# Splitting the preparation of a seven-product unit among the down chunks of a feed-forward kernel

## The chip, the core and the metric

The kernel runs on one core of one Trainium2 chip. The metric is the device time of one execution in microseconds (us); less is better. The core has TensorE (PE in the profile, with PEld for its weight loads), VectorE (DVE), ScalarE (ACT), GpSimd (POOL) and SyncE (SP, which here only issues DMA transfers). Every engine works through its own queue strictly in the order in which the program was written down; a semaphore wait at the head of a queue holds up all that stands behind it.

## What is computed

One encoder layer over 512 tokens with a model width of 1024. Two feed-forward half steps (hidden width 2816) stand around an attention mixer, and a gated embedding closes the layer:

```
h = h + 0.5 * swiglu(rms_norm(h, g_ffn1), w_ffn1_gate, w_ffn1_up, w_ffn1_down)
u = rms_norm(h, g_mix) @ w_in
...                                       # two kinds of attention on parts of u
h = h + concat([o_mla, o_diff]) @ w_out
h = h + 0.5 * swiglu(rms_norm(h, g_ffn2), w_ffn2_gate, w_ffn2_up, w_ffn2_down)
gate = sigmoid(rms_norm(h, g_ple_in) @ w_ple_gate + b_ple_gate)
h = h + gate * rms_norm(p @ w_ple_proj, g_ple_out)

swiglu(u, wg, wu, wd) = (silu(u @ wg) * (u @ wu)) @ wd
```

All weights come in float32. The kernel keeps float32 accuracy by splitting each operand into a high part and a low part and making three matmuls for each product (lines 391, 392 and 393: high by high, high by low, low by high).

## The kernel before

**Feed-forward, groups.** A feed-forward step works through its 22 hidden blocks of 128 in four groups (`FGROUPS`): a first, *plain* group of 4 blocks and three groups of 6. Every group makes its hidden blocks `ht` (gate product, silu, times up product) and then runs the *down* stage: eight products `ps_d`, one for each output block m, each added into `h[m]` at line 677.

**Units.** In the groups of 6 the gate and up products are not made directly: `seven` multiplies a 2 by 2 arrangement of weight blocks with 2 by 2 parts of the activations in seven products of 12 matmuls each (three partial sums in PSUM, `r1`, `r2`, `r3`) instead of eight. One `Unit` holds the weights of one such call. Units alternate: one for the gate of a pair of hidden blocks, one for the up. A group has 6 units, the kernel 36. A unit is prepared in 11 steps:

- loads on SP: `rb` and `rc` (`load_b`), then `ra` (`load_a`);
- `sums` (lines 157 and 158): two transfers issued by POOL, which add another weight block from memory onto `rb` and `rc`;
- `cast_a`, `cast_b` (ACT, lines 162, 166): high parts of `xa` and `xb`; `low_a`, `low_b` (DVE, line 97): their low parts. `low_b` also has POOL add `rb` into `ra` in two steps (lines 174, 175), which can't begin before `low_a` has read `ra`;
- `cast_c`, `low_c` for `xc`; `cast_s0`, `low_s0`, `cast_s1`, `low_s1` (ACT lines 187, 193, DVE line 97) for the two halves of `xs`, made from the summed `ra`.

The first product of `seven` needs the first half of `xs`: its high part for the matmuls of lines 391 and 392, its low part for line 393.

**Order.** The list `items` holds all weights in the order of use: the plain weights as `Chunk` (one load, one cast, one low part), the units, and the down chunks behind the units of their group. `advance` takes the next step of the front item. It is called by `steps(n)` inside `seven`, between its products (1, 2, 2, 1, 1, 2, 2 steps, so 11 for each unit), and by `slot(us)` elsewhere, until a budget of time is spent, a unit is ready, or the buffers (`held`, three of each kind) are full. Loads run ahead of the steps through three raw buffers (`RAWS`). So a step's place in the queues is where `steps` or `slot` stood when it was taken. In the down stage of the kernel before, `slot` and then `build(2)` stand behind the update of `h[m]` at line 677. `build` hands out the preparation of the activations (`Forms`: `y` at line 499, the sums at lines 506 to 515, `sa` and `fm` pages), which has to be over before the first unit.

**End.** After the last group eight gate chunks (`ps_pg`) follow, whose results `evac_gate` finishes on DVE and ACT. Before each group of `evac_gate` calls stands a `slot`, partly behind them.

## Time and profile before

| | |
|---|---|
| time, median of 3 runs | 1118.36 us (1117.15 to 1119.0) |
| time of the profiled execution | 1119.93 us |
| span of the profiled execution (first to last instruction) | 1118.2 us |
| PE busy | 1039.0 us (93% of the span) |
| DVE, ACT, POOL busy | 769.2, 522.5, 324.9 us |
| mean granted TensorE clock | 0.984 of full speed |
| chain that ended last, by engine | PE 55%, DVE 21%, issue 7%, ACT 5%, DMA 3% |

The profile is of one execution. Its time is 1.6 us above the median of the three timed runs and 1.7 us above its own span. PE is idle for 79 us of the span; a busy PE counts matmuls from their start to their modelled end, which overlap.

### The profile page before, as it was taken

What the parts mean: (1) busy time and instruction counts of PE and PEld (TensorE: products, weight loads), DVE (VectorE), ACT (ScalarE), POOL (GpSimd) and SP (SyncE); (2) the same over time, 40 slices, a digit from 0 to 9 for tenths busy, and PEclk for the clock granted to TensorE, in tenths of its full rate; (3) what the DMA queues carried; (4) which work ended last, traced back from release to release, by engine and by line L of the source; (5) the groups of instructions that cost most, each with busy time, mean ns of one, the idle gap of its engine ahead of it and who ended that gap; (6) DMA issues with size and microseconds to landing.
All of it is one profiled execution on the core that took longest, in us unless ns stands there. A gap on an engine that the chain in (4) does not pass through costs nothing.

```text
span 1118.2 us, 16005 instructions
## 1 busy us (share of the span) xinstructions
PE 1039.0 (93%) x6100; PEld 904.9 (81%) x6100; DVE 769.2 (69%) x1277; ACT 522.5 (47%) x891; POOL 324.9 (29%) x283
## 2 busy tenths in 40 slices
PE   8978899889988999999999999978898889989998
PEld 7768888878888898876667888778887888888777
DVE  7796754775567558888798763977745674677765
ACT  6443442443344346568687552534433442344432
POOL 1133312440433110026553231234325330452000
PEclk9998999999999999999999999989999999999999
DMA  7254635554554443222112122255465635555231
GB/s 244 79 136 128 141 114 144 148 132 149 131 145 112 136 147 129 76 81 77 51 40 70 39 94 76 85 132 145 119 214 138 152 109 142 151 141 180 84 105 67
DMA packets 50463, 133.76 MB, mean 120 GB/s; under 512 B 5873, under 2 KB 6897, under 8 KB 50385
## 3 DMA queue, kind: packets, MB, share of 16 engines
q1 hardware_dynamic: 37008, 106.88, 28.9%
q0 software_dynamic: 11792, 23.47, 11.9%
q10 hardware_dynamic: 1584, 2.39, 0.6%
q8 instruction: 48, 0.79, 0.3%
q14 instruction: 31, 0.25, 0.1%
HBM read 126.02 MB, written 6.29 MB: 118 GB/s over the span
## 4 chain that ended last, share of the span: by engine, by line
PE 55%; DVE 21%; issue 7%; ACT 5%; DMA 3%; POOL 1%; DVEq 0%; SPq 0%; ACTq 0%; POOLq 0%
PE r L393 7%; PE r L391 5%; PE r L392 5%; PE ps_d L391 5%; PE ps_d L392 5%; PE ps_d L393 5%; DVE xb L97 3%; DVE q L559 3%; PE ps_in L392 2%; PE ps_in L391 2%; PE ps_in L393 2%; DVE xs L97 2%; DVE xc L97 2%; DVE hl L97 2%; PE ps_wo L391 1%
## 5 line engine op out<-in xcount | busy, mean ns | idle before, releaser
L97 DVE TENSOR_TENSOR hl<-raw,hl 128x1024 fp32r<-128x1024 f32 (+4 forms) x110 | 121.4, 1114 | 47.0 <-ACT hl L124 44.8
L174 POOL TENSOR_TENSOR ra<-ra,rb 128x512 f32<-128x512 f32 x36 | 76.7, 2130 | 249.5 <-DVE xa L97 247.0
L124 ACT CAST hl<-raw 128x1024 fp32r<-128x1024 f32 (+2 forms) x104 | 96.5, 942 | 108.3 <-DMA raw<-in_wst_dram 35.0
L393 PE MATMUL ps_d<-ht,hl 128*128 128x512 f32 x352 | 137.4, 390 | 2.3 <-DVE hl L97 2.3
L392 PE MATMUL ps_d<-ht,hl 128*128 128x512 f32 x352 | 137.3, 390 | 0.2
L391 PE MATMUL ps_d<-ht,hl 128*128 128x512 f32 x352 | 137.3, 390 | 0.0
L391 PE MATMUL r<-sa,xa 128*128 128x256 f32 x288 | 84.2, 292 | 0.0
L392 PE MATMUL r<-sa,xa 128*128 128x256 f32 x288 | 84.2, 292 | 0.0
L393 PE MATMUL r<-sa,xa 128*128 128x256 f32 x288 | 84.0, 292 | 0.0
L391 PE MATMUL r<-fm,xb 128*128 128x256 f32 x288 | 82.0, 285 | 0.0
L392 PE MATMUL r<-fm,xb 128*128 128x256 f32 x288 | 81.7, 284 | 0.0
L393 PE MATMUL r<-fm,xb 128*128 128x256 f32 x288 | 81.5, 283 | 0.0
L393 PEld LDWEIGHTS ps_d<-ht,hl 128*128 128x128 f32 x352 | 66.1, 188 | 17.6 <-DVE hl L97 4.0
L97 DVE TENSOR_TENSOR xs<-ra,xs 128x512 fp32r<-128x512 f32 x72 | 52.0, 725 | 40.8 <-ACT xs L193 22.1
L391 PE MATMUL r<-fm,xs 128*128 128x256 f32 x144 | 44.4, 309 | 37.2 <-ACT xs L187 37.2
L392 PEld LDWEIGHTS ps_d<-ht,hl 128*128 128x128 f32 x352 | 66.1, 188 | 14.5 <-DVE ht L94 1.0
L391 PEld LDWEIGHTS ps_d<-ht,hl 128*128 128x128 f32 x352 | 66.1, 188 | 13.4
L555 DVE TENSOR_TENSOR q<-r,q 128x256 f32<-128x256 f32 x36 | 15.3, 425 | 79.1 <-PE r L393 75.8
L393 PE MATMUL r<-fm,xs 128*128 128x256 f32 x144 | 46.3, 321 | 24.7 <-DVE xs L97 24.7
L391 PEld LDWEIGHTS r<-fm,xs 128*128 128x128 f32 x144 | 28.8, 200 | 42.2 <-ACT xs L187 42.1
L157 POOL DMA_DIRECT2D rb<-in_wst_dram x36 | 31.8, 884 | 91.0 <-DMA rb<-in_wst_dram 61.1
L392 PEld LDWEIGHTS r<-sa,xa 128*128 128x128 f32 x288 | 58.1, 202 | 0.0
(335 smaller groups left out, 3150.4 us busy)
## 6 DMA issues: line engine op xcount, KB each, us to landing
raw<-in_wst_dram SPq DMA_DIRECT2D x52, 512.0 KB, 3.5
rb<-in_wst_dram SPq DMA_DIRECT2D x36, 512.0 KB, 4.1
ra<-in_wst_dram SPq DMA_DIRECT2D x36, 512.0 KB, 3.4
raw<-in_wst_dram SPq DMA_DIRECT2D x48, 384.0 KB, 3.5
rc<-in_wst_dram SPq DMA_DIRECT2D x36, 256.0 KB, 4.4
rb<-in_wst_dram POOLq DMA_DIRECT2D x36, 256.0 KB, 4.5
rc<-in_wst_dram POOLq DMA_DIRECT2D x36, 256.0 KB, 5.6
h<-in_xT_dram SPq DMA_DIRECT2D x8, 256.0 KB, 4.4
```

Source lines behind the costliest of these rows:

```text
L97: nc.vector.tensor_sub(dst_l, src, dst_h.bitcast(F32))
L124: nc.scalar.copy(self.hl[:, 0, :self.n], self.raw[:, :self.n])
L157: nc.gpsimd.dma_start(out=self.rb[:, self.LO], in_=self.s1[:, self.HI], accum_op=ALU.add)
L174: nc.gpsimd.tensor_add(ra[:, LO], ra[:, LO], self.rb[:, LO])
L391: MM(ps, lhsT=wh, rhs=ah, start=start, stop=False, **kw)
L392: MM(ps, lhsT=wh, rhs=al, start=False, stop=False, **kw)
L393: MM(ps, lhsT=wl, rhs=ah, start=False, stop=stop, **kw)
L555: nc.vector.tensor_add(q2[:, lo], r3[:, lo], q1[:, lo])
L559: nc.vector.tensor_sub(q1[:, hi], q1[:, lo], q2[:, hi])
```

## The change

It has five parts.

1. The order of a unit's steps becomes `cast_a`, `low_a`, `cast_b`, `low_b` (before: both casts, then both low parts).
2. The first unit of a group is taken apart: its loads and `sums` (one `Part`) and its next four steps (a second `Part`) stand among the down chunks of the group before, with cut 2, 2 in the plain group and 6, 7 in the others; the other six steps stay behind the chunks. The source addresses are taken when an item is made, so that the order of use no longer sets them.
3. `slot` goes on over a ready unit if the next step is the `sums` of a whole unit. In the `seven` of a group's first unit the steps therefore begin with `cast_a` of the second, and all stand one step earlier.
4. In the down stage `slot` stands ahead of the update of `h[m]`, and `build` is spread out (one step in each of the three early products of the plain group, one for m below 2, then two).
5. At the end, four of the eight gate chunks use the other kind of buffer, and `slot(3.0)` stands ahead of the `evac_gate` calls.

```diff
     class Unit:
-            self.steps = [(0.0, self.sums, 0), (0.1, self.cast_a, 1), (0.1, self.cast_b, 1), (1.2, self.low_a, 0),
+            self.steps = [(0.0, self.sums, 0), (0.1, self.cast_a, 1), (1.2, self.low_a, 0), (0.1, self.cast_b, 1),
                           (1.2, self.low_b, 0), (0.1, self.cast_c, 0), (0.7, self.low_c, 0),
...
+    class Part:
+
+        def __init__(self, unit, n, loads):
+            self.which = unit.which
+            self.loads = [unit.loads.pop(0) for _ in range(loads)]
+            self.steps = [unit.steps.pop(0) for _ in range(n)]
+
     def ffn_items():
...
+                down = [Chunk(2 * n * P) for m in range(0, KT, 2)]
+                cut = 2, 2
             else:
+                items.extend(first_unit if u == 0 else Unit(1 - u % 2) for u in range(n))
+                down = [Chunk(n * P, 1 if m < KT // 2 else 0) for m in range(KT)]
+                cut = 6, 7
+            if gi < len(FGROUPS) - 1:
+                first_unit = Unit(1)
+                early_ = Part(first_unit, 1, 2), Part(first_unit, 4, 0)
+                down.insert(cut[1], early_[1])
+                down.insert(cut[0], early_[0])
+            items.extend(down)
...
-    items.extend(Chunk(BLK) for _ in range(KT))
+    items.extend(Chunk(BLK, 1 if m < KT // 2 else 0) for m in range(KT))
...
-        while st["time"] > 0 and not any(isinstance(it, Unit) for it in ready) and advance():
+        while st["time"] > 0 and (not any(isinstance(it, Unit) for it in ready)
+                                  or isinstance(items[-1], Unit) and len(items[-1].steps) == 11) and advance():
             pass
...
                     slot(1.3)
+                    build(1)
...
+                slot(0.0 if plain and m < 2 else 0.68 * n - (2.2 if gi == len(FGROUPS) - 1 else 0.75))
                 nc.vector.scalar_tensor_tensor(out=h[m], in0=ps, scalar=0.5, in1=h[m],
                                                op0=ALU.mult, op1=ALU.add)
...
-                slot(0.0 if plain and m < 2 else 0.68 * n - (2.2 if last else 0.75))
-                build(2)
+                build(1 if m < 2 else 2)
...
+        slot(3.0)
         if m == 1:
             rbc = row_bcast(r4)
-            slot(1.2)
         for e in pend:
             evac_gate(*e)
         pend = []
-        slot(3.0)
```

The lines of the changed kernel inside `ffn` and `seven` are numbered 17 higher than those of the kernel before (555 becomes 572); those of `Unit` and of the helpers stay.

**DVE, an up unit (the second of a pair).** Of the kernel before, from the result of its third product (line 555) to the first half of `xs` of the next unit:

```order
L555 TENSOR_TENSOR q_848<-r_846,q_847 128x256
L97 TENSOR_TENSOR xa<-ra,xa 128x1024
L97 TENSOR_TENSOR xb<-rb,xb 128x1024
L558 TENSOR_TENSOR q_849<-r_845,q_848 128x256
L559 TENSOR_TENSOR q_847<-q_847,q_848 128x256
L604 TENSOR_TENSOR a_719<-r_844,a_719 128x256
L97 TENSOR_TENSOR xc<-rc,xc 128x512
L565 TENSOR_TENSOR q_848<-r_846,q_847 128x256
L604 TENSOR_TENSOR a_719<-q_848,a_719 128x256
L97 TENSOR_TENSOR xs<-ra,xs 128x512
```

The same place in the changed kernel:

```order
L97 TENSOR_TENSOR xa<-ra,xa 128x1024
L572 TENSOR_TENSOR q_850<-r_848,q_849 128x256
L97 TENSOR_TENSOR xb<-rb,xb 128x1024
L575 TENSOR_TENSOR q_851<-r_847,q_850 128x256
L576 TENSOR_TENSOR q_849<-q_849,q_850 128x256
L97 TENSOR_TENSOR xc<-rc,xc 128x512
L621 TENSOR_TENSOR a_721<-r_846,a_721 128x256
L582 TENSOR_TENSOR q_850<-r_848,q_849 128x256
L621 TENSOR_TENSOR a_721<-q_850,a_721 128x256
L97 TENSOR_TENSOR xs<-ra,xs 128x512
```

The low part of `xa` stands ahead of the third product's result, and that of `xc` ahead of the fifth's; the first half of `xs` stands where it stood.

**ACT, a gate unit (the first of a pair).** Of the kernel before, from the cast of `xc` to the second half of `xs` (lines 597 and 599 are the silu of the three partial results):

```order
L180 CAST xc<-rc 128x512
L597 ACTIVATE a_719<-r_720 128x256
L597 ACTIVATE a_719<-q_724 128x256
L187 CAST xs<-ra 128x512
L599 ACTIVATE q_725<-q_725 128x512
L193 CAST xs<-ra 128x512
```

The same place in the changed kernel:

```order
L180 CAST xc<-rc 128x512
L614 ACTIVATE a_721<-r_722 128x256
L187 CAST xs<-ra 128x512
L614 ACTIVATE a_721<-q_726 128x256
L193 CAST xs<-ra 128x512
L616 ACTIVATE q_727<-q_727 128x512
```

Each cast of `xs` stands one silu earlier.

**DVE, the end of the plain group.** Of the kernel before; `hl` is the low part of a down chunk, lines 584 to 588 make the last hidden block, whose low part is `ht`:

```order
L97 TENSOR_TENSOR hl<-raw,hl 128x1024
L584 TENSOR_TENSOR a<-ps_g,rbc 128x512
L587 TENSOR_TENSOR v<-ps_u,rbc 128x512
L588 TENSOR_TENSOR v<-a,v 128x512
L94 TENSOR_TENSOR ht<-v,ht 128x512
```

The same place in the changed kernel:

```order
L97 TENSOR_TENSOR hl<-raw,hl 128x1024
L97 TENSOR_TENSOR xa<-ra,xa 128x1024
L97 TENSOR_TENSOR xb<-rb,xb 128x1024
L601 TENSOR_TENSOR a<-ps_g,rbc 128x512
L604 TENSOR_TENSOR v<-ps_u,rbc 128x512
L605 TENSOR_TENSOR v<-a,v 128x512
L94 TENSOR_TENSOR ht<-v,ht 128x512
```

The low parts of `xa` and `xb` of the next group's first unit stand ahead of the last hidden block of the plain group. On ACT the casts of both stand ahead of that block's silu in the same way, and on SP the loads of `rb`, `rc` and `ra` ahead of those of the last two down chunks. On POOL the order inside a group is the same in both kernels: lines 174 and 175 of a unit, then lines 157 and 158 of the next.

## Rows read from the trace of the kernel before

**Rows 1.** PE's waits, whole span: engine line <- released by: us, times, longest.

```profile
PE r L391 <- ACT xs L187: 37.2, 21, 4.4
PE r L393 <- DVE xs L97: 24.7, 33, 1.9
```

**Rows 2.** PE's waits, 76 to 86 us: the first unit of the first feed-forward.

```profile
PE r L391 <- ACT xs L187: 4.4, 1, 4.4
PE r L393 <- DVE xs L97: 1.9, 1, 1.9
```

**Rows 3.** PE's waits, 840 to 856 us: first unit behind the embedding's norm.

```profile
PE r L391 <- ACT xs L187: 1.1, 1, 1.1
```

**Rows 4.** Timeline, PE, 107.9 to 114: start, us, engine line op out<-in [idle <-releaser].

```profile
110.65 0.28 PE L392 MATMUL r<-fm,xs 128*128 128x256 f32 x1
112.32 0.39 PE L393 MATMUL r<-fm,xs 128*128 128x256 f32 x1 [1.39 <-DVE xs L97]
```

**Rows 5.** Stretches: us, busy (instructions) of PE PEld DVE ACT POOL, PEclk, DMA share, GB/s.

```profile
98.40:110.41 12.01, 11.79 (x83) 11.58 (x84) 7.07 (x10) 4.92 (x8) 3.65 (x3) 0.86 0.49 117
191.35:201.31 9.96, 9.96 (x85) 9.95 (x83) 6.18 (x8) 3.56 (x6) 4.09 (x4) 1.00 0.55 118
889.80:901.81 12.01, 11.79 (x83) 11.58 (x84) 7.06 (x10) 4.90 (x8) 3.64 (x3) 0.86 0.47 105
```

**Rows 6.** Timeline, DVE, an up unit; the last row is without POOL beside it.

```profile
105.04 0.42 DVE L555 TENSOR_TENSOR q<-r,q 128x256 f32<-128x256 f32 x1 [3.74 <-PE r L393]
105.39 1.22 DVE L97 TENSOR_TENSOR xa<-ra,xa 128x1024 fp32r<-128x1024 f32 x1
...
107.99 1.18 DVE L559 TENSOR_TENSOR q<-q,q 128x256 f32<-128x256 f32 x1
...
109.43 1.45 DVE L97 TENSOR_TENSOR xc<-rc,xc 128x512 fp32r<-128x512 f32 x1
...
111.58 0.68 DVE L97 TENSOR_TENSOR xs<-ra,xs 128x512 fp32r<-128x512 f32 x1
...
1025.47 0.41 DVE L559 TENSOR_TENSOR q<-q,q 128x256 f32<-128x256 f32 x1
```

**Rows 7.** Timeline, POOL, beside the same up unit.

```profile
106.69 2.20 POOL L174 TENSOR_TENSOR ra<-ra,rb 128x512 f32<-128x512 f32 x1 [8.47 <-DVE xa L97]
108.97 1.35 POOL L175 TENSOR_TENSOR ra<-ra 128x512 f32<-128x512 f32 x1
110.27 0.86 POOL L157 DMA_DIRECT2D rb<-in_wst_dram  x1
```

**Rows 8.** Timeline, ACT, the gate unit behind it.

```profile
122.97 0.42 ACT L597 ACTIVATE a<-q 128x256 f32<-128x256 f32 x1 [3.00 <-DVE q L565]
123.29 0.60 ACT L187 CAST xs<-ra 128x512 fp32r<-128x512 f32 x1
```

**Rows 9.** Landing, 110 to 111 us: issue, KB each, us from issue to landing.

```profile
rb<-in_wst_dram POOLq DMA_DIRECT2D x1, 256.0 KB, 4.3
```

**Rows 10.** Timeline, end of the first plain group: SP, ACT, then DVE.

```profile
55.65 0.33 SPq L120 DMA_DIRECT2D raw<-in_wst_dram  x1
...
68.92 1.05 ACT L162 CAST xa<-ra 128x1024 fp32r<-128x1024 f32 x1 [2.78 <-DMA ra<-in_wst_dram]
...
58.47 0.69 DVE L584 TENSOR_TENSOR a<-ps_g,rbc 128x512 f32<-128x512 f32 x1
...
74.98 1.73 DVE L94 TENSOR_TENSOR sa<-y,sa 128x512 fp32r<-128x512 f32 x1 [1.84 <-ACT sa L93]
...
83.78 0.68 DVE L97 TENSOR_TENSOR xs<-ra,xs 128x512 fp32r<-128x512 f32 x1
```

**Rows 11.** Landing of the load issued at 55.65: issue, KB, us from issue to landing.

```profile
raw<-in_wst_dram SPq DMA_DIRECT2D x1, 512.0 KB, 3.3
```

**Rows 12.** PE's waits, 1050 us to the end: the last stage.

```profile
PE ps_pg L393 <- DVE hl L97: 1.7, 2, 0.9
PE ps_d L393 <- DVE hl L97: 0.6, 1, 0.6
```

More of the change, by code (lines that the diff above doesn't have):

```diff
@@ L113, in __init__ @@
         def __init__(self, n, which=0):
-            self.n, self.which = n, which
+            self.n, self.which, self.src = n, which, take(n)
             self.loads = [self.load]
@@ L119, in load @@
             self.raw = raw_tile()
-            nc.sync.dma_start(out=self.raw[:, :self.n], in_=take(self.n))
+            nc.sync.dma_start(out=self.raw[:, :self.n], in_=self.src)
         def cast(self):
@@ L139, in __init__ @@
             self.which = which
+            self.s0, self.s1 = take(BLK), take(BLK)
             self.loads = [self.load_b, self.load_a]
-            self.steps = [(0.0, self.sums, 0), (0.1, self.cast_a, 1), (0.1, self.cast_b, 1), (1.2, self.low_a, 0),
+            self.steps = [(0.0, self.sums, 0), (0.1, self.cast_a, 1), (1.2, self.low_a, 0), (0.1, self.cast_b, 1),
                           (1.2, self.low_b, 0), (0.1, self.cast_c, 0), (0.7, self.low_c, 0),
@@ L146, in load_b @@
         def load_b(self):
-            self.s0, self.s1 = take(BLK), take(BLK)
             self.rb, self.rc = raw_tile("rb"), t2("rc")
@@ L203, in release @@
             held[self.which] -= 3
+    class Part:
[3 more added lines that the diff above has]
+            self.steps = [unit.steps.pop(0) for _ in range(n)]
     items = []
     def ffn_items():
-        for f0, n, plain in FGROUPS:
+        first_unit = None
+        for gi, (f0, n, plain) in enumerate(FGROUPS):
             if plain:
                 items.extend(Chunk(BLK) for _ in range(2 * n))
-            else:
-                items.extend(Unit(1 - u % 2) for u in range(n))
-            if plain:
-                items.extend(Chunk(2 * n * P) for m in range(0, KT, 2))
-            else:
-                items.extend(Chunk(n * P, 1 if m < KT // 2 else 0) for m in range(KT))
+                down = [Chunk(2 * n * P) for m in range(0, KT, 2)]
+                cut = 2, 2
+            else:
+                items.extend(first_unit if u == 0 else Unit(1 - u % 2) for u in range(n))
[7 more added lines that the diff above has]
+            items.extend(down)
     ffn_items()
@@ L247, in advance @@
         if not it.steps:
-            ready.append(items.pop())
+            items.pop()
+            if not isinstance(it, Part):
+                ready.append(it)
         load_ahead()
@@ L408, in encoder_layer @@
         loads.pop()
-        it.raw, it.hl, it.src = raw_tile(), hl_tile(0), take(BLK)
+        it.raw, it.hl = raw_tile(), hl_tile(0)
         held[0] += 1
```

## The prediction
> **What bounds the kernel now.** I read PE's waits first. PE is idle for 79 us, and 61.9 of them are two waits of one kind [rows 1]: the first product of a unit waits for the high part of `xs` (ACT, 37.2 us in 21 waits) and then for its low part (DVE, 24.7 us in 33). So nearly all that PE loses is lost at the start of units. Then I read the same view in short windows, to part the waits. The first unit of a feed-forward waits 4.4 and 1.9 us [rows 2], the first unit behind the embedding's norm 1.1 us and a little for the low part [rows 3]; with the other feed-forward's first unit taken to be like that of rows 2, the first units hold some 9.6 us of the waits for ACT and 4 of those for DVE. What is left, some 48 us, is in the 30 changes from one unit to the next inside the groups, 5 in each of 6 groups. The reader sees one such change in the timeline [rows 4]: line 392 runs, line 393 begins 1.67 us later, where matmuls of this kind follow each other every 0.12 us (84 in 9.96 us [rows 5]). The view counts 1.39 us, since it starts from the modelled end of the matmul before (0.28 us long). So each wait costs 0.16 us more than it shows; over some 48 waits that is 7.7 us, and the changes cost 48 + 8 = 56 us.
>
> Two patterns alternate. Up to gate: DVE comes late. In an up unit its queue runs without a pause from the third product's result to `xs` [rows 6]: the result at 105.04 comes after 3.74 us of idling, and then `xa`, `xb` and `xc`, which waited for nothing but their turn, are worked off between the results. On top of that the adds of POOL fall into this stretch [rows 7], and DVE operations that read two operands from SBUF stretch beside them: line 559 takes 1.18 us where it takes 0.41 alone, `xc` 1.45 where `xs`, of the same size, takes 0.68 [rows 6]. Gate to up: ACT comes late, because the cast of `xs` stands behind the silu of the sixth product, and that silu behind DVE [rows 8]. These are the waits for ACT: (37.2 - 9.6) / 18 = 1.5 us each, and 0.2 behind them for the low part, 2.1 us with the 0.16 twice (18 changes, 37 us). Up to gate costs the 1.55 us of rows 4 (12 changes, 19 us).
>
> **The changes between units.** The loads, sums, casts and adds are the same in number; only places move. On ACT the cast of `xs` goes ahead of that silu. Seven products are 1.44 us each (12 times 0.12). Counted from the moment at which the third product's result can be read, the sixth's can be read at 4.32 and PE wants the low part of `xs` at about 5.8 (the seventh product, then two matmuls). In a gate unit DVE then does the sixth product's sum (0.4) and `xs` (0.7): ready at 5.4, so that change costs nothing, if DVE isn't late by more than 0.4. In an up unit there is a multiplication more (0.4): ready at 5.8. DVE is late there by what POOL takes from it. The queue between is: result 0.35, `xb` 1.13, two sums 0.7, `xc` 0.6, multiplication 0.35, about 3.15 us by the steps between starts; `xa` now runs in the 3.74 us in which DVE idled. That leaves 4.32 - 3.15 = 1.2 us for POOL's two adds. From below they cost nothing (the slack takes 1.2 us of them); from above both add their whole stretch, 0.77 twice on line 559 and `xc` as now, and 0.4 on `xb`, which makes 1.9 and leaves 0.7 us late. I take 0.4, nearer to the row with POOL beside it: 12 times 0.4 = 5 us stay of 56. **Gain 51 us.**
>
> This needs the data in time. POOL's queue keeps its order: two adds, then the two transfers of the next unit's sums, with what waits behind them the same. From the first add to the issue pass 3.6 us (106.69 to 110.27 [rows 7]) and to the landing 4.3 more [rows 9], so the loop over POOL takes 8 us, against a unit of 10.08. The first add follows `xa`, whose cast now stands behind the first product's copy: some 4.4 us into the unit. The sums then land 4.4 + 7.9 - 10.1 = 2.2 us into the next, a microsecond before ACT reaches the cast of `xb`. The cover is 1 to 2 us wide; if it is gone, ACT waits in front of that cast, and `xs` behind it.
>
> The rows show DVE and POOL taking turns on such operations [rows 6, 7]. The Trainium skill says so too (SBUF — State Buffer, "Who interferes with whom"): a DVE instruction with two SBUF inputs and a GpSimd instruction that reads SBUF exclude each other for the whole instruction. By that rule both adds would always be paid in full, 0.7 us would stay at each of the 12 changes, and the sum would be 3.6 us worse.
>
> **The clock.** Four units that are not first in a group run at a granted clock of 0.86, a stretch of them at 1.2 instead of 2.4 GHz [rows 5]; the rows are the first and the last of the four. They take 12.01 us; less 9.96 and the 0.4 of the wait inside, each loses 1.7 us. All of them begin right behind a wait for `xs`. From below nothing comes back, from above 6.8 us. Two of the four are the second units of the first-unit groups, behind the long wait that I keep in another form below. **I take 5 us.**
>
> **The first unit of each feed-forward.** It is ready earlier, but its preparation now stands in front of the plain group's last hidden block on ACT and DVE. The load of `ra` takes the place of the load issued at 55.65 [rows 10], since that raw buffer comes free there, and lands 3.3 us later [rows 11], at 58.9. Then the cast, 1.05 us [rows 10], `xa` and `xb` on DVE, 1.2 and 1.1: DVE turns to the last hidden block at 62.3, or 63.4 if POOL's add comes between, instead of 58.47 [rows 10]. PE needs that block for the fourth part of its down products, behind 27 matmuls that need only the first three; these end about when the block is ready now, for the view of rows 1 has no wait for `ht`. So a new wait of 3.8 to 4.9 us stands in the plain group. On the other side the wait of rows 2 goes, if `xs` is ready when the down products end. From the last hidden block to `xs` DVE's queue takes 25.3 us now (58.47 to 83.78 [rows 10]); it loses `xa` and `xb` (2.3), two updates of h that fall behind `xs` (1.2), and the pause and the slow `sa` (1.84 and 1.05 [rows 10]): 19 us. So `xs` starts at 81.3 to 82.4 instead of 83.78, and PE goes on 1.4 to 2.5 us earlier. The two down chunks that the unit is moved past on SP load when the next raw buffers come free, at 58.6 and about 63.5, land by 67 and are wanted by PE at about 71 and 76, so that their move costs nothing; without that cover each would add its lateness. Twice, in the two feed-forwards, with 2 each: **gain 4 us**; from below 0, if the ends add up badly. The long idle time stays in a new place; as now, a stretch at the lower clock may follow it.
>
> **The first unit behind the norm of the embedding** loses its wait, since its sums now stand ahead of the norm's adds in POOL's queue: 1.1 us [rows 3], with the wait for the low part and the restart **2 us**. The first units of the other groups wait for nothing now and are prepared earlier.
>
> **The end.** Three waits for `hl`, 1.7 and 0.6 us [rows 12] and 0.16 each: the chunks' low parts now stand ahead of the updates and of `evac_gate`. **Gain 2.5 us** of 2.8. What is put behind them, the updates of h and the gates, is waited for by no matmul within the next product; PE is what ends last there.
>
> **Sum.** 51 + 5 + 4 + 2 + 2.5 = 64.5 us. Against the profiled execution's 1119.9 us that is 1055.4; it lies 1.6 above the median, so the forecast is 1054 us.
>
> **Rivals.** (1) POOL and DVE pay each other in full, or DVE gets behind for another reason, and the up-to-gate waits stay as they are: 13.8 us more, and the clock gives nothing back, 5 more: 1073 us, up to 1082 if gate-to-up keeps 0.5 of its 2.1 us. For it: DVE's queue in the up unit has no pause from the third result on [rows 6], and units would be shorter. Against: the 3.74 us before it are idle, and `xa` moves there.
> (2) The change doesn't do in the units what it says, because the sums' landing, not the order, sets `xs`. Then the 56 us and the clock stay, and only 8.5 us go: 1110 us. Against it: casts follow each other on ACT, and the wait in [rows 8] is for DVE.
> (3) Slower: the loop over POOL. More traffic in less time lengthens the landing; with 3.6 us from add to issue it sets the unit's time from 6.5 us on, and equals today's mean of 12 us (10.08 and 56/30) from 8.4. At 9.5 each of 36 units takes 13.1 us: 36 times 1.1 = 40 us more, 1150 us with the other gains (8.5). Against: 4.3 us [rows 9] and a DMA share of only 0.49 to 0.55 [rows 5].
>
> **How the numbers follow.** Forecast 0.63 (its own range 1043 to 1067), rival 1 0.22, rival 2 0.05, rival 3 0.04; the rest, 0.06, is a better clock or fewer waits than I take, down to 1042, and cases between rivals 1 and 2. The range is 1042 to 1082: the forecast and most of rival 1. A difference of 0.2% is about what a measurement of this kernel can tell from no change. Faster by more than that are the forecast, rivals 1 and 2 and the rest: 0.94; within it 0.02, rival 2 with a dear plain group; slower 0.04.
>
> **What would show it.** In the changed profile the waits for `xs` by ACT should be gone but for a first unit, those by DVE at or below 0.7 us, 12 of them; the stretch of a unit should be 10 to 10.5 us; a new wait of 3.5 to 5 us for `ht` should stand in each plain group; the waits for `hl` at the end should be gone. I am wrong if units take over 11 us, if ACT waits for a DMA before the cast of `xb`, or if PE's new wait in the plain group is over 6 us.

## The result and the profile after

The changed kernel takes 1062.99 us (median of 4 runs, 1061.28 to 1066.2) against 1118.35 us in the same comparison: ratio 0.951, 95% interval [0.949, 0.953]. The forecast was 1054 us, the range 1042 to 1082. By the medians that is 55.4 us less. The profiled execution took 1061.3 us, its span is 1059.5 (1118.2 before); it was the fastest of the four, and that of before lies 1.6 us above its median, so the two spans differ by more, 58.7 us.

PE's waits over the whole span of the changed kernel (lines of the functions concerned are 17 higher than before: 408 is 391, 410 is 393), as in [rows 1] and [rows 12]:

```profile
PE ps_d L408 <- ACT ht L93: 13.5, 2, 7.5
PE ps_ss L364 <- POOL pe_acc L354: 5.9, 1, 5.9
PE ps_d L410 <- DVE hl L97: 1.8, 2, 0.9
...
PE ps_pg L408 <- ACT act_ple_in L396: 0.4, 1, 0.4
...
PE ps_pg L409 <- DVE act_ple_in L397: 0.3, 1, 0.3
```

The reader sees that no wait for `xs` is among the lines of the view any more, where there were 61.9 us. Two waits for `ht` stand in the plain groups, as forecast, but longer; the wait of 5.9 us for `pe_acc` was not forecast at all; the three waits for `hl` at the end are gone, for two small ones.

Next, stretches between the first matmuls of the stages: us, busy time (instructions) of PE, PEld, DVE, ACT and POOL, granted clock, DMA share, GB/s. First the kernel before: down products of the first plain group, the six units of the second group with units, and the down stage with the embedding's norm.

```profile
54.18:82.08 27.90, 22.55 (x98) 17.68 (x96) 25.27 (x34) 13.47 (x21) 10.72 (x8) 1.00 0.48 118
...
191.35:262.05 70.70, 62.54 (x505) 60.90 (x504) 49.84 (x71) 31.06 (x54) 25.12 (x19) 1.00 0.56 141
...
818.28:853.25 34.97, 33.83 (x154) 27.66 (x152) 14.90 (x21) 12.62 (x20) 15.82 (x13) 1.00 0.54 166
```

The same three stretches after the change:

```profile
52.14:84.75 32.61, 24.20 (x97) 18.90 (x96) 27.25 (x35) 13.81 (x21) 10.91 (x8) 0.90 0.50 129
...
178.77:239.79 61.02, 60.99 (x506) 60.57 (x505) 47.76 (x70) 31.32 (x54) 24.10 (x18) 1.00 0.57 148
...
775.78:817.89 42.11, 36.21 (x155) 29.81 (x154) 20.66 (x23) 12.76 (x20) 18.88 (x14) 0.92 0.59 171
```

A group of six units takes 61.0 us instead of 70.7, at a clock of 1.00, and PE is busy in 60.99 of them. The two other stretches became longer, with a granted clock of 0.90 and 0.92 where it was 1.00.

Read so for all stages, the 58.7 us of the two spans lie here (stages not listed, the down stages between, differ by 0.0):

| stage | before | after | difference |
|---|---|---|---|
| to the first down product | 54.18 | 52.14 | -2.0 |
| first feed-forward: plain down products and six units | 104.5 | 94.0 | -10.5 |
| its other two groups of units | 142.8 | 122.0 | -20.7 |
| third down stage, attention, up to the second feed-forward's first down product | 347.8 | 349.0 | +1.2 |
| second feed-forward: plain down products and six units | 103.7 | 93.3 | -10.4 |
| down stage with the embedding's norm | 35.0 | 42.1 | +7.1 |
| the other two groups of units | 143.3 | 122.0 | -21.3 |
| last down stage and end | 89.0 | 86.9 | -2.1 |

The first row is in part the profiled run of before itself: its granted clock is at the lower level from 7.8 to 11.2 us, and that of the run after is not.

**A change from up to gate.** PE's timeline (start, us, engine, line), which answers to [rows 4]:

```profile
105.31 0.28 PE L409 MATMUL r<-fm,xs 128*128 128x256 f32 x1
105.66 0.39 PE L410 MATMUL r<-fm,xs 128*128 128x256 f32 x1
```

The first matmul with the low part of `xs` comes 0.35 us behind the one before it, where it was 1.67 and where 0.12 is the usual distance, so 0.23 us of the wait are left (0.17 at the same place in the second group with units). DVE's queue around this change and in the gate unit behind it (that of [rows 6] is an up unit), with the idle time ahead of an operation in brackets:

```profile
104.92 0.69 DVE L97 TENSOR_TENSOR xs<-ra,xs 128x512 fp32r<-128x512 f32 x1
...
108.57 1.23 DVE L97 TENSOR_TENSOR xa<-ra,xa 128x1024 fp32r<-128x1024 f32 x1
110.11 0.42 DVE L572 TENSOR_TENSOR q<-r,q 128x256 f32<-128x256 f32 x1 [0.31 <-PE r L410]
110.45 1.81 DVE L97 TENSOR_TENSOR xb<-rb,xb 128x1024 fp32r<-128x1024 f32 x1
...
112.52 1.18 DVE L576 TENSOR_TENSOR q<-q,q 128x256 f32<-128x256 f32 x1
```

The low part of `xs` is done at 105.61, just before PE's matmul at 105.66. `xa` now stands ahead of the third product's result (line 572), and DVE has idle time in the unit again (0.31 us ahead of that line). POOL's adds still cost DVE something: `xb` takes 1.81 us where `xa`, of the same size, takes 1.23, and line 576 takes 1.18 where it takes 0.41 without POOL [rows 6]: 1.4 us in all. In the up unit ahead of the change the two take 1.80 and 1.17 us. The slack takes all of that but the 0.2 us at the change.

**The wait for `ht`.** In the first plain group, the landings of the loads and sums issued at 51 to 54 us (queue, KB, us from issue to landing), then ACT, then DVE:

```profile
ra<-in_wst_dram SPq DMA_DIRECT2D x1, 512.0 KB, 6.4
rb<-in_wst_dram POOLq DMA_DIRECT2D x1, 256.0 KB, 4.9
rc<-in_wst_dram POOLq DMA_DIRECT2D x1, 256.0 KB, 7.3
```

```profile
60.01 1.04 ACT L162 CAST xa<-ra 128x1024 fp32r<-128x1024 f32 x1 [6.05 <-DMA ra<-in_wst_dram]
...
66.50 0.62 ACT L93 CAST ht<-v 128x512 fp32r<-128x512 f32 x1 [1.79 <-DVE v L605]
```

```profile
61.09 1.22 DVE L97 TENSOR_TENSOR xa<-ra,xa 128x1024 fp32r<-128x1024 f32 x1 [4.57 <-ACT xa L162]
62.23 1.22 DVE L97 TENSOR_TENSOR xb<-rb,xb 128x1024 fp32r<-128x1024 f32 x1
63.36 0.68 DVE L601 TENSOR_TENSOR a<-ps_g,rbc 128x512 f32<-128x512 f32 x1
...
64.75 1.72 DVE L605 TENSOR_TENSOR v<-a,v 128x512 f32<-128x512 f32 x1
...
84.45 1.28 DVE L97 TENSOR_TENSOR xs<-ra,xs 128x512 fp32r<-128x512 f32 x2
```

The load of `ra` is issued at 53.61 and lands 6.4 us later, not 3.3 as that of [rows 11]; the two transfers of the unit's sums, issued at 51.29 and 52.07, are in flight with it. In the second feed-forward the same load lands in 4.7 us, and PE's wait is 5.9 us there. A chunk's load that is issued 2.9 us behind `ra` isn't the reason: the load of [rows 11] has one as far behind it. ACT stands for 6.05 us in front of the cast, DVE for 4.57, and line 601 of the last hidden block comes at 63.36. Then line 605 takes 1.72 us beside POOL's adds, where it took 0.69. The high part of `ht` is cast at 66.50; PE's wait of 7.5 us in the first view ends with it. In the last row, the low part of `xs` starts at 84.45; unit 0 begins at 84.75.

**The wait for `pe_acc`.** POOL's timeline ahead of it:

```profile
785.86 0.89 POOL L157 DMA_DIRECT2D rb<-in_wst_dram  x1 [22.33 <-DMA rb<-in_wst_dram]
...
791.39 1.30 POOL L354 TENSOR_TENSOR pe_acc<-pe_acc,sq 128x512 f32<-128x512 f32 x1 [3.74 <-ACT sq L353]
...
797.13 1.28 POOL L174 TENSOR_TENSOR ra<-ra,rb 128x512 f32<-128x512 f32 x1
...
799.74 6.55 POOL L354 TENSOR_TENSOR pe_acc<-pe_acc,sq 128x512 f32<-128x512 f32 x4
```

ACT's, of the same stretch:

```profile
789.42 0.84 ACT L124 CAST hl<-raw 128x768 fp32r<-128x768 f32 x1 [6.98 <-DMA raw<-in_wst_dram]
```

PE's four small matmuls (line 364) stand in its queue behind the one of 800.07 and need the last of the adds of line 354, which end at 806.3. That is 30.5 us into the stage; in the kernel g1 below, which prepares this unit whole and has no such wait, it is 24.0. Two things make the difference. The norm's adds begin 4.2 us later in the stage: on ACT their squares stand behind the cast of a down chunk, and that cast waits 6.98 us, for a load which now stands behind the unit's `rb` and `ra`. And from 792.92 on POOL has no pause, so that the unit's two adds, put between the norm's, come on top with 2.7 us; beside DVE's work the norm's own seven adds take 12.1 us where they take 10.0 in g1.

### The profile page after: what moved, and what is told of

Read it like the earlier page. It is cut to its first block, busy times and chain, and to the rows that moved or that the text cites. A ratio compares the mean times of both kernels' runs of the same rounds, so it can differ in the third digit from the quotient of the medians.

```text
span 1059.5 us, 16005 instructions
## 1 busy us (share of the span) xinstructions
PE 1026.2 (97%) x6100; PEld 899.0 (85%) x6100; DVE 762.8 (72%) x1277; ACT 524.3 (49%) x891; POOL 325.1 (31%) x283
## 4 chain that ended last, share of the span: by engine, by line
PE 81%; DVE 8%; ACT 4%; DMA 4%; issue 2%; POOL 1%; SPq 0%; ACTq 0%; DVEq 0%; POOLq 0%
PE r L410 11%; PE r L408 11%; PE r L409 11%; PE ps_d L408 7%; PE ps_d L409 6%; PE ps_d L410 6%; PE ps_in L408 2%; PE ps_in L410 2%; PE ps_in L409 2%; DVE hl L97 1%; PE ps_pt L1160 1%; PE ps_wo L408 1%; PE ps_wo L410 1%; PE ps_wo L409 1%; PE ps_pg L409 1%
## 5 line engine op out<-in xcount | busy, mean ns | idle before, releaser
L408 PE MATMUL ps_d<-ht,hl 128*128 128x512 f32 x352 | 140.3, 398 | 13.5 <-ACT ht L93 13.5
L410 PE MATMUL ps_d<-ht,hl 128*128 128x512 f32 x352 | 139.1, 395 | 1.8 <-DVE hl L97 1.8
L409 PE MATMUL ps_d<-ht,hl 128*128 128x512 f32 x352 | 139.5, 396 | 0.0
L174 POOL TENSOR_TENSOR ra<-ra,rb 128x512 f32<-128x512 f32 x36 | 48.3, 1341 | 224.2 <-DVE xa L97 216.2
L408 PEld LDWEIGHTS ps_d<-ht,hl 128*128 128x128 f32 x352 | 67.6, 192 | 28.1 <-ACT ht L93 14.3
L410 PEld LDWEIGHTS ps_d<-ht,hl 128*128 128x128 f32 x352 | 67.4, 192 | 16.8 <-DVE hl L97 2.6
L408 PE MATMUL r<-sa,xa 128*128 128x256 f32 x288 | 81.5, 283 | 0.0
L409 PE MATMUL r<-sa,xa 128*128 128x256 f32 x288 | 81.5, 283 | 0.0
L410 PE MATMUL r<-sa,xa 128*128 128x256 f32 x288 | 81.5, 283 | 0.0
L409 PEld LDWEIGHTS ps_d<-ht,hl 128*128 128x128 f32 x352 | 67.6, 192 | 14.7 <-DVE ht L94 0.9
L175 POOL TENSOR_TENSOR ra<-ra 128x512 f32<-128x512 f32 x36 | 75.0, 2084 | 2.8
L97 DVE TENSOR_TENSOR xa<-ra,xa 128x1024 fp32r<-128x1024 f32 x36 | 44.3, 1231 | 38.7 <-ACT xa L162 38.7
L97 DVE TENSOR_TENSOR xb<-rb,xb 128x1024 fp32r<-128x1024 f32 x36 | 63.1, 1753 | 0.0
L408 PEld LDWEIGHTS r<-sa,xa 128*128 128x128 f32 x288 | 55.3, 192 | 0.0
L409 PEld LDWEIGHTS r<-sa,xa 128*128 128x128 f32 x288 | 55.3, 192 | 0.0
L410 PEld LDWEIGHTS r<-sa,xa 128*128 128x128 f32 x288 | 55.3, 192 | 0.0
```

Of the source, the lines that this page charges most:

```text
L97: nc.vector.tensor_sub(dst_l, src, dst_h.bitcast(F32))
L174: nc.gpsimd.tensor_add(ra[:, LO], ra[:, LO], self.rb[:, LO])
L175: nc.gpsimd.tensor_add(ra[:, HI], ra[:, HI], ra[:, LO])
L408: MM(ps, lhsT=wh, rhs=ah, start=start, stop=False, **kw)
L409: MM(ps, lhsT=wh, rhs=al, start=False, stop=False, **kw)
L410: MM(ps, lhsT=wl, rhs=ah, start=False, stop=stop, **kw)
```

## The experiments

All are compared with the kernel before on the same chip in the same job.

| run | edit | median, us | ratio to before, 95% |
|---|---|---|---|
| the change | | 1062.99 | 0.951 [0.949, 0.953] |
| e1_step_only | before, and the slot's condition | 1057.64 | 0.945 [0.942, 0.948] |
| e2_no_step | the change without that condition | 1116.61 | 0.998 [0.997, 1.000] |
| e3_hold | plain group: second part behind the last hidden block | 1053.81 | 0.943 [0.940, 0.946] |
| e4_pe_late | the norm's matmuls two chunks later | 1053.36 | 0.942 [0.939, 0.945] |
| f1_hold_pe | both | 1046.68 | 0.936 [0.933, 0.938] |
| f2_plain_whole | plain groups: first unit whole | 1059.66 | 0.947 [0.945, 0.950] |
| f3_old_slot | slot behind the update of h | 1063.87 | 0.952 [0.949, 0.954] |
| f4_old_tail | end as before | 1061.54 | 0.949 [0.946, 0.952] |
| g1_others_whole | other groups: first unit whole | 1054.21 | 0.941 [0.939, 0.944] |
| g2_cut23_pe | as e4, second part one chunk later | 1050.15 | 0.938 [0.936, 0.940] |
| h1_loads_late_pe | as g2, the unit's loads one chunk later | 1046.89 | 0.936 [0.934, 0.939] |

**The one condition alone, and everything but it.**

```diff
-        while st["time"] > 0 and not any(isinstance(it, Unit) for it in ready) and advance():
+        while st["time"] > 0 and (not any(isinstance(it, Unit) for it in ready)
+                                  or items and isinstance(items[-1], Unit) and len(items[-1].steps) == 11) and advance():
```

> The kernel before with one thing of the change: the condition in `slot` that lets the sums of the next unit go while a whole unit stands ready, so that every step in `seven` stands one place earlier. Theory A (the one step sets the changes between units by itself): the waits for xs inside the groups go, a unit takes 10.0 to 10.3 us, the four units at a clock of 0.86 get it back; that is 54 + 6 us of 1118.4, so 1058 us (1054 to 1066), while the first units still wait 4.4 and 1.9 us for xs and the end for hl. Theory B (the step needs the first unit in parts and the slot ahead of the update as well, since otherwise DVE comes into the units late): waits for xs of 0.5 to 1.5 us stay in most of the 30 changes, 1075 to 1100 us.

Measured 1057.6 us: theory A. A group of units takes 61.02 us, as with the whole change. PE's waits for `xs` in the whole span of this kernel (line 392 is 408 of the changed one, 394 is 410):

```profile
PE r L392 <- ACT xs L187: 10.6, 3, 4.4
PE r L394 <- DVE xs L97: 5.1, 4, 1.6
```

What is left are the first units of the feed-forwards and of the group behind the embedding's norm (4.4, 4.2 and 2.0 us by the first row's three waits), and besides these one wait of 1.5 us at a change from up to gate in the second feed-forward. So one line brings more than the whole change: the other parts together cost 5 us, and the two intervals lie apart. There is no wait for `pe_acc` in this kernel, and POOL's timeline shows why:

```profile
796.88 2.67 POOL L338 TENSOR_TENSOR pe_acc<-pe_acc,sq 128x512 f32<-128x512 f32 x2 [0.22 <-ACT sq L337]
...
803.17 0.90 POOL L157 DMA_DIRECT2D rb<-in_wst_dram  x1
```

The last of the norm's adds end at 799.6, and the next unit's sums come behind them, with none of a unit's operations between.

> The changed kernel with that condition alone undone; first units in parts, slot ahead of the update and the end stay changed. Theory A: the waits for xs of 1.4 and 1.5 us come back at the 30 changes, 54 us and 5 of the clock, 1063 + 59 = 1122 us (1108 to 1126), a little slower than the kernel before because the waits for ht and pe_acc (13.5 and 5.9 us) come on top and the ones of the first units go. Theory B (the other parts bring the units into step): 1063 to 1085 us.

Measured 1116.6 us: theory A again, and better than its sum by 5. The waits for `xs` are back in nearly all changes:

```profile
PE r L408 <- ACT xs L187: 22.9, 18, 1.3
PE r L410 <- DVE xs L97: 21.7, 30, 1.5
```

A group of units takes 70.0 us. Without the step the other four parts together bring 0.2%.

**The second part held back in the plain group.** A flag is set while the plain loop runs and cleared behind the last evacuation:

```diff
-        if held[it.which] + tiles > 3:
+        if held[it.which] + tiles > 3 or hold[0] and isinstance(it, Part) and len(it.steps) == 4:
             return False
```

> The changed kernel, but in the plain group the four steps of the first unit (casts and low parts of xa and xb, with POOL's two adds) are held back until the last hidden block is evacuated. Theory A (DVE's queue sets when the first unit starts; it has only 4.57 and 2.91 us of idling there, plus about a microsecond on the blocked product of line 605): the waits for ht of 7.5 and 5.9 us go, but waits for xs of 2 to 4 us stand in front of units 0 and 18 again; gain about 5.5 and 3.9, 9.4 us, so 1053.6 us (1051 to 1057). Theory B (nothing but the wait for ht stood there): PE gets back both waits, the restarts and the slow clock behind them, 7.5 + 5.9 + 0.7 + 1.7 + 3.1 = 18.9 us, 1044 us. Theory C (the wait only moves, the whole stretch is as long): 1062 to 1063 us.

Measured 1053.8 us, theory A: 9.2 us come back of the 18.9 that theory B counts. Plain down products and six units take 90.0 and 90.9 us instead of 94.0 and 93.3. Only the place of the new wait was not as I had written: it stands for the most part in front of two down chunks, which now come behind `xa` and `xb` (below), and 0.5 us in front of unit 0.

**The norm's matmuls later.**

```diff
-                    for _ in range(2):
+                    for _ in range(2 if m < 3 else 1):
                         next(side, None)
```

> The changed kernel, but the side work pe_norm goes on by one step instead of two behind the updates of h from m = 3 on, so that the sums of its squares (ps_ss, matmuls with pe_acc) stand two down chunks, 8.6 us, further on in PE's queue; the adds into pe_acc stay where they are in POOL's queue. Theory A (PE is simply there too early: the adds end at 806.3 us, PE comes at 800.1): the wait of 5.9 us goes, and the stretch at half clock behind it (804.5 to 811.4) with it, 5.9 + 0.3 + up to 2.5: 1054.3 to 1056.8 us. Theory B (what is late there is the preparation for the next group's first unit, and the wait only hid it): the first unit behind then waits 5 us or more for xs, 1061 to 1063 us; against it xs is ready at 806.8, 11 us before that unit begins.

Measured 1053.4 us: theory A, with a microsecond more than its upper price. The stretch of that down stage:

```profile
774.95:808.43 33.48, 33.48 (x155) 27.85 (x153) 20.61 (x22) 12.82 (x20) 18.39 (x13) 1.00 0.71 210
```

PE is busy in all of its 33.48 us, at full clock: 8.6 us less than in the changed kernel, 1.5 less than before. The first unit behind it waits for nothing. The edit moves one thing more than PE's matmuls: the last of the norm's adds now stands behind the next unit's sums on POOL. It ends at 807.1, 0.5 us before PE's matmuls begin.

**First unit whole in the other groups.** The two parts are made for the plain groups alone.

```diff
-            if gi < len(FGROUPS) - 1:
+            first_unit = None
+            if plain:
                 first_unit = Unit(1)
```

> The changed kernel with the first unit in parts in the plain groups alone; in the other groups it is prepared whole behind the down chunks, as before. Theory A (the wait for pe_acc comes from the parts: the unit's sums and adds stand between the adds into pe_acc in POOL's queue, and its loads ahead of those of pel): the wait for pe_acc goes, as in the kernel with the one condition alone, and the first unit behind it waits some 2 us for xs again; its down stage takes 35.8 us instead of 42.1, so 1063.0 - 6.3 = 1056.7 us (1055 to 1058.5). Theory B (it comes from the slot ahead of the update): the wait stays, 1062 to 1064 us.

Measured 1054.2 us, theory A and somewhat better:

```profile
775.93:809.55 33.62, 33.62 (x154) 27.94 (x153) 16.00 (x21) 13.41 (x20) 16.85 (x14) 1.00 0.61 182
```

33.62 us, and the first unit behind it doesn't wait (0.06 us) although it is prepared whole. So outside the plain groups the parts bring nothing that the rest of the change doesn't bring, and without them the wait for `pe_acc` is gone. (With the condition alone this unit waited 2.0 us; which of the other edits removes that was not run.)

**Both.**

> The changed kernel with both edits together: the four steps of the first unit held back in the plain group, and pe_norm slower from m = 3 on. They stand in different places (the plain groups; the second group of the second feed-forward). Theory A (two separate costs): the gains measured apart, 9.2 and 9.6 us, add up: 1063.0 - 18.8 = 1044.2 us (1042.5 to 1046). Theory B (the earlier PE in the plain group brings the work of the next groups closer together, and one gain eats the other): 1048 to 1053 us.

Measured 1046.7 us against a kernel before that took 1119.4 in this job, 1.4 us more than in the one before. The 1046.7 us lie between the ranges of the two theories, 0.7 us above that of A. The ratio, 0.936, is between what the two gains give when added up (0.934) and the one alone (0.942); in the profiled spans (1059.5, 1051.4, 1051.6 and 1043.7 us) they add up within 0.2 us. So theory A, nearly in full, and this kernel beats both. PE's waits in it from 52 to 92 us, one row of POOL's timeline, and DVE's timeline:

```profile
PE ps_d L410 <- DVE hl L97: 3.4, 3, 2.0
PE ps_d L408 <- ACT hl L124: 1.4, 1, 1.4
PE r L410 <- DVE xs L97: 0.5, 1, 0.5
```

```profile
64.33 5.20 POOL L174 TENSOR_TENSOR ra<-ra,rb 128x512 f32<-128x512 f32 x1 [9.49 <-DVE xa L97]
```

```profile
64.17 0.75 DVE L516 SCALAR_TENSOR_TENSOR y<-h,gc,rbc 128x512 f32<-128x512 f32 x1
...
68.30 0.68 DVE L696 SCALAR_TENSOR_TENSOR h<-ps_d,h 128x512 f32<-128x512 f32 x1
...
74.48 1.22 DVE L97 TENSOR_TENSOR hl<-raw,hl 128x1024 fp32r<-128x1024 f32 x1 [2.69 <-ACT hl L124]
```

POOL's add on line 174 takes 5.20 us, where its mean in the changed kernel is 1.34. From 64.17 to 68.3 five operations of DVE with two operands in SBUF follow each other without a pause. The update of `h` at 68.30 reads one of its two from PSUM; from its start to the end of the add, at 69.53, pass 1.2 us, about what the add takes alone. So the add seems to have had no turn among the five. The add reads the raw buffer into which the last down chunk is loaded, and DVE idles 2.69 us until it has that chunk, at 74.48.

**First unit whole in the plain groups.** The same condition the other way round (`and not plain`).

> The changed kernel with the first unit of the two plain groups prepared whole behind the down chunks, as before; in the other groups it stays in parts. Theory A (moving the parts in front of the last hidden block costs more than the earlier unit gives): the waits for ht go, a wait for xs of some 4 us comes back in front of units 0 and 18, with POOL's adds and the casts of xs directly behind xb; between the 1053.8 us with the steps held back and the 1057.6 us with the one condition alone, 1056 us (1053 to 1060). Theory B (my forecast for this step, a gain of 2 us in each plain group): 1067 us.

Measured 1059.7 us: at the upper end of theory A, far from B. Waits in front of unit 0:

```profile
PE r L410 <- DVE xs L97: 2.9, 1, 2.9
PE r L408 <- ACT xs L187: 1.4, 1, 1.4
```

Plain products and units take 91.9 and 91.9 us, 2.1 and 1.4 less than with the parts as the change makes them, and 1.9 and 1.0 more than with the second part held back. So by these profiles my gain in the plain groups was a loss, and the idea is good only if the second part doesn't stand ahead of the last hidden block. The intervals of the three ratios just touch, so the times alone would not decide it.

**The slot behind the update of h again.**

```diff
-                slot(0.0 if plain and m < 2 else 0.68 * n - ...)
                 nc.vector.scalar_tensor_tensor(out=h[m], in0=ps, scalar=0.5, in1=h[m],
...
+                slot(0.0 if plain and m < 2 else 0.68 * n - ...)
```

> The changed kernel with the slot behind the update of h again, two builder steps behind each update and none in the loop over the first three down products. In the plain group six updates of h then stand ahead of the low part of xs in DVE's queue instead of four. Theory A (DVE's queue sets the start of units 0 and 18, which is without slack in the trace: xs low at 84.45, unit 0 at 84.75): 2 times 0.6 us in each, 1.2 to 2.4 us each, 1065.4 to 1068 us. Theory B (the place of the updates is hidden): 1062 to 1064 us.

Measured 1063.9 us: theory B by the time. The profiles don't agree on the plain groups (92.6 and 94.6 us against 94.0 and 93.3), so a difference of a microsecond either way stays open.

**The end as before.**

```diff
-    items.extend(Chunk(BLK, 1 if m < KT // 2 else 0) for m in range(KT))
+    items.extend(Chunk(BLK) for _ in range(KT))
...
-        slot(3.0)
         if m == 1:
             rbc = row_bcast(r4)
+            slot(1.2)
         for e in pend:
             evac_gate(*e)
         pend = []
+        slot(3.0)
```

> The changed kernel with the end as before: the last chunks all in the first buffer pool, the slots behind evac_gate. Theory A (the three waits for hl at the end cost what they show, 1.7 + 0.6 us and the restarts): 2.5 us slower, 1065.5 us. Theory B (they are taken up by the end of the last gate product and its stores): no difference, 1063 us.

Measured 1061.5 us: theory B, though not for the reason it gives. Only one of the three waits is back, against 0.4 and 0.3 us for `act_ple_in` in the changed kernel:

```profile
PE ps_pg L410 <- DVE hl L97: 0.9, 1, 0.9
```

Last down stage and end take 89.0 us before, 88.9 with the step alone, 87.6 with the slot behind the update, 87.2 with this end, 86.9 with the whole change. By these profiles, one of each kernel, either of the two edits brings most of the 2 us by itself; the ratios can't tell them apart.

The other order of casting (`low_a` ahead of `cast_b`) was not run alone: beside the rest it only swaps two neighbouring operations on DVE (the low part of `xa` and an update of `h`), once in each of four down stages.

**Can the plain group be better still?** In the plain groups alone, with the norm's matmuls later as in e4. For h1 the two parts take 0 and 2 loads there in place of 2 and 0.

```diff
-                cut = 2, 2
+                cut = 2, 3
```

> The changed kernel with pe_norm slower from m = 3 on, and in the plain group the second part of the first unit behind the third down chunk instead of the second (a 3 for a 2): its casts and low parts then fall behind the last hidden block of themselves, and the chunk, for which PE waited 2.0 us in each plain group with the steps held back, is cast ahead of xa and xb. Theory A (DVE's queue up to xs sets the start of units 0 and 18, whatever its order): the wait for that chunk goes and 1 to 2 us of waiting come back at the next chunk or at xs, no difference to 1046.7 us (1045 to 1048). Theory B (the wait for the chunk was on top): 2 us less in each plain group, 1042.7 us.

> As the run before with the second part behind the third down chunk and pe_norm slower, but in the plain groups the unit's loads (rb, rc, ra) stand behind the third chunk's load too, and its sums still ahead of its casts. There the fourth chunk's load takes the raw buffer of the third chunk (free when that is cast and its low part taken, some 64 us) instead of that of rb, which POOL's first add held until 69.5 in the kernel with the steps held back (line 174 took 5.20 us there) and longer in the run before. Theory A (the wait of 5.1 us for the fourth chunk comes from that buffer): the wait goes, DVE has no pause between sa and that chunk, and each plain group takes 4 to 5 us less than in the run before: 1050.2 - 9 = 1041 us (1040 to 1045). Theory B (rb is loaded 7 us later, so that the sums land behind ACT's turn for xb, and ACT stands): a pause of the same size on ACT and DVE, 1047 to 1053 us.

Measured 1050.2 and 1046.9 us; their intervals overlap with each other and with that of both edits above. In g2 the wait for the third chunk goes and 5.1 us come in front of the fourth: the mechanism of theory A, but the wait only moved and grew, and the time is above the range of either theory. In h1 the time lies between the two ranges, and neither mechanism came. The wait is still 5.0 us, though the buffer is free early: the fourth chunk is cast at 67.80, as theory A wanted, and its low part starts at 74.73. PE's waits in h1 from 52 to 92 us, ACT's row, then DVE's:

```profile
PE ps_d L410 <- DVE hl L97: 5.8, 2, 5.0
```

```profile
67.80 1.05 ACT L124 CAST hl<-raw 128x1024 fp32r<-128x1024 f32 x1 [1.48 <-DMA raw<-in_wst_dram]
```

```profile
63.89 1.77 DVE L516 SCALAR_TENSOR_TENSOR y<-h,gc,rbc 128x512 f32<-128x512 f32 x1
...
66.72 1.77 DVE L94 TENSOR_TENSOR sa<-y,sa 128x512 fp32r<-128x512 f32 x1
68.42 2.31 DVE L97 TENSOR_TENSOR xb<-rb,xb 128x1024 fp32r<-128x1024 f32 x1
70.65 1.75 DVE L94 TENSOR_TENSOR sa<-y,sa 128x512 fp32r<-128x512 f32 x1
...
74.73 1.21 DVE L97 TENSOR_TENSOR hl<-raw,hl 128x1024 fp32r<-128x1024 f32 x1
```

DVE has no pause. Beside POOL's four operations the builder's operations and `xb` take 1.77, 1.77, 2.31 and 1.75 us, where 0.68 to 1.22 is what they take alone, and the chunk stands behind them. So what I took for the cause in h1, the raw buffer, isn't it: DVE's own queue is full, as in g2's theory A, and the three orders that were run only pick who waits. In this kernel `ra` is loaded with the sums issued a microsecond behind it, not two ahead:

```profile
ra<-in_wst_dram SPq DMA_DIRECT2D x1, 512.0 KB, 3.2
```

## Why the prediction came out as it did

**What bounds the kernel** was read rightly: nearly all that PE lost was at the changes between units, and all but some 4 us of that is gone.

**The changes.** Direction and mechanism were right, the size too small. In the group without a first wait and at full clock, 70.70 us became 61.02: 9.7 us for five changes, 58 for thirty, where I had 51. I had put the cost at 56; six units of 9.96 us with 0.12 between them are 60.36, so by the same group it was 10.34 times 6, 62 us. What the sum of 48 waits and 0.16 us each left out stands behind each wait. In the change of [rows 4] the matmul behind the late one, at 112.32, is this:

```profile
112.55 0.28 PE L391 MATMUL r<-fm,xs 128*128 128x256 f32 x1
```

It comes 0.23 us later and not 0.12, as behind each of the eight waits of the second group with units; 0.1 us for 48 waits is 5 of the 6 us. What stays is 0.66 us in a group, 4 us in all, for the 5 that I kept. POOL's adds cost DVE 1.4 us a unit (I had 0 to 1.9). The prediction weighed a rule of the Trainium skill (SBUF — State Buffer, "Who interferes with whom"), by which such instructions exclude each other for the whole instruction. The trace agrees that DVE's operations stretch (1.81 for 1.23 us), but of the 0.7 us that I derived from it only some 0.2 stay at a change, for DVE has slack in front of the result.

**The clock.** The four units of 12.01 us are gone, so all of the 6.8 us came back there, where I took 5. But the granted clock is now 0.90 and 0.89 in the two plain stages and 0.92 behind the norm, each behind a long wait of PE. I had said that such a stretch may follow the wait in its new place, and had given it no price.

**The first unit of each feed-forward: wrong in sign.** I had a gain of 2 us each. Of the 10.5 and 10.4 us that these stages gained, five changes are 9.7 and the clock of the second unit 1.7; the first unit itself lost 0.8 and 1.0 us. By my own sign, a wait of over 6 us in the plain group, this step is wrong: the waits were 7.5 and 5.9 us for 3.8 to 4.9. Three terms failed. The first is the landing. I took 3.3 us from a load without sums beside it, and this one took 6.4, in the second feed-forward 4.7. It was issued 1.5 us into the stage, as that of [rows 11] was; so DVE came to the last hidden block 11.2 us into the stage (63.36 less 52.14), where my sum has 8.1, or 9.2 with POOL's add between (62.3 and 63.4 less 54.18). That 63.36 is so close to 63.4 is chance: the changed run begins the stage 2 us earlier, and POOL's add did not come between. The second is the block itself, which I let take as long as before: line 605 stood behind POOL's adds for 1.0 us. From 3.8 us these two make 7.9 and 6.2, near the 7.5 and 5.9. The third is DVE's queue from there to `xs`: 21.1 us (63.36 to 84.45), where I had 19. That DVE's queue is what sets this stage, as I had argued, is what e3, f2, g2 and h1 show: whatever the order, PE waits there for DVE's `hl` or `xs`.

**The first unit behind the embedding's norm: wrong in sign, and the largest miss.** I had seen that the unit's sums pass the norm's adds on POOL's queue and counted the gain for the unit, 2 us. I didn't ask who waits for the adds that they pass: PE, with four matmuls in the middle of the down stage; nor what the unit's loads pass on SP, which is the chunk that ACT casts ahead of the norm's squares. The stage lost 7.1 us. In e4 and in g1 the wait is gone, and the stage takes 33.5 and 33.6 us.

**The end** was right in sum (2.1 for 2.5). I had put it down to the low parts standing ahead of the updates and of `evac_gate`, both together; by f3 and f4 either of the two moves brings most of it alone.

**The sum.** By the two spans, 58.7 us instead of 64.5: 7 more at the changes, 2 more of the clock, 2 in the start, against 6 less in the plain groups, 9 less at the norm and 1 to 2 elsewhere. The forecast was near because errors of both signs met. None of the rivals came: POOL's price was covered but for some 0.2 us at a change, the step set `xs`, and the sums landed in time (in 36 casts of `xb`, ACT waits for a DMA for 1.9 us in all).

## What to carry to other kernels

When work is moved ahead in a queue, list what it passes and who waits for that; the dearest miss here was a side computation of four tiny matmuls, whose adds got two others in between and whose inputs came behind two more loads. A part of a preparation moved in front of a result that PE needs soon costs its slowest input, with the landing it has beside its own traffic, not that of a load that runs alone. And test the parts of a change apart: here one condition carried all of the gain, and the others paid only once two places had been put right, the second part of the first unit in the plain groups and the norm's matmuls (1046.7 us for the 1057.6 of the one condition).

## What the hardware showed that I had not expected

POOL can be kept out for several DVE operations in a row: the add on line 174 took 5.20 us in f1_hold_pe while DVE worked back to back, against a mean of 1.34, and in the other order (h1) DVE's operations of 0.68 us took 1.75 to 1.77. Who gets the next turn was not tested. A load of 512 KB took 4.7 to 6.7 us to land in the plain groups of the nine kernels that issue the unit's two accumulating transfers 0.6 to 2.7 us ahead of it, and 3.2 and 3.5 us in h1, which issues them about a microsecond behind it; a load at that place with none beside it took 3.3 to 3.5 us, in the kernel before and in f2. Only the order of issue and the landing are measured; how the transfers share the DMA engines was not.
